# A quarter of the down projection by seven block products in place of eight

## The chip, the cores and the metric

The kernel runs on one core of a Trainium2 chip. The metric is the device time of one launch in microseconds (us), as the median of several runs. The engines are named as in the profile: PE is TensorE (PEld its weight loads), DVE is VectorE, ACT is ScalarE, POOL is GpSimd and SP is SyncE, whose queue issues the loads.

## The reference

One layer of an encoder trunk on 256 tokens of width 2048, in float32. After a combined input projection, three branches (a bidirectional state-space scan, a dilated windowed attention, a convolution module) are gated and merged. Then follows the part that this case is about, the MLP with 8192 hidden columns:

```python
x = x + merged @ w_out[i]
h2 = rms_norm(x, norm2_g[i])
x = x + jnp.square(jax.nn.relu(h2 @ w_mlp_up[i])) @ w_mlp_down[i]
```

## The kernel before

All large products are made in one stream of *units*. A unit is 256 rows of a weight matrix times 512 output columns: one load of 128 x 1024 floats (512 KB, tile `raw`, five buffers). Every operand is carried as two parts of type `fp32r`: ACT copies `raw` into `hi`, and DVE subtracts to make `lo = raw - hi` (`split_lo`, L254). Both have four buffers, and `split` runs `LEAD` = 3 units ahead of the matmuls (`mm`). A product a x w is then three matmuls: a_hi w_hi and a_lo w_hi (first all those that read `hi`), then a_hi w_lo.

In a unit of the down projection ("X" mode) the activations are the stationary operand: the 256 rows are two chunks e of 128, the 256 tokens two halves t, so 2 x 2 x 3 = 12 matmuls of 512 columns. They accumulate in a `main` tile of two PSUM banks (one for each t). In the up projection ("W" mode) the weights are stationary, 24 matmuls of 256 columns.

A *block* is eight units with one accumulator: 2048 rows of K, 512 output columns. The MLP is cut into r = 0 to 3, each with 2048 hidden columns: four up blocks ("U", r, i), then four down blocks ("D", r, i) over K of 2048, in the order U0 U1 D0 U2 D1 U3 D2 D3. When an up block is done, `job_up` has DVE apply relu and the norm (`u`, L1075, two instructions), ACT square it and copy it to `ah`, and DVE split off `al`. When a down block is done, `job_down` adds its two banks into `oacc[i]` (tile `x` in the traces) on DVE (L1095), or for r = 3 adds and stores the output (L1099).

What the engines do in which order is fixed when the program is built. The loop over units writes down, for unit k, the load of k + 5, the split of k + 3 and the matmuls of k. Then `S.tick` lets waiting jobs write some of their instructions, against a credit of free DVE and ACT time. Each engine executes its own queue in order and waits on semaphores. PSUM has eight banks: the pool `pm` gives two `main` tiles (four banks), the pool `pd` four single banks for everything else; the last block of all takes two of `pd`. `S.require` makes the planner write a reader's instructions before the buffer is given out again.

Of the kernel before, what the change touches and what calls it, by code (L numbers as in the profile page):

```python
# [12 lines left out]
F32 = mybir.dt.float32  # L13
# [7 lines left out]
P = 128  # L21
# [169 lines left out]
def kernel(ctx: ExitStack, tc: tile.TileContext, xT, xn, par, cm, cd, cq, w1, wq, ws, out):  # L191
# [869 lines left out]
        st["rbc2"] = rb  # L1061


    act = {}

    def job_up(main, r, i):
        yield "m", 3
        u = slab([4, T], name="u")
        h = slab([4, T], F32R, name="ah")
        l = slab([4, T], F32R, name="al")  # L1070
        yield "j", lambda: "rbc2" in st
        yield "w", 1
        for e in range(2):
            yield "v", 680
            V.scalar_tensor_tensor(u[:, 2 * e:2 * e + 2, :], main[:, e, :].rearrange("p (a b) -> p a b", a=2), 0.0,  # L1075
                                   st["rbc2"][:, None, :].to_broadcast([P, 2, T]), op0=ALU.max, op1=ALU.mult)
        st["main_free"].add(id(main))
# [7 lines left out]
        S.give()  # L1085
        act[r][0][i] = h
        act[r][1][i] = l

    def job_down(main, r, i):
        if r < 3:  # L1090
            yield "j", lambda: oacc[i] is not None
            yield "w", 1
            for t in range(2):
                yield "v", 620
                V.tensor_tensor(oacc[i][:, t, :], oacc[i][:, t, :], main[:, t, :], op=ALU.add)  # L1095
            st["main_free"].add(id(main))
            return
        for t in range(2):
            V.tensor_tensor(oacc[i][:, t, :], oacc[i][:, t, :], main[:, t, :], op=ALU.add)  # L1099
            (nc.sync, nc.scalar)[t].dma_start(out[t * P:t * P + P, i * 512:i * 512 + 512], oacc[i][:, t, :])  # L1100
        st["main_free"].add(id(main))
        yield "w", 0


    st.update(h=([None] * 4, [None] * 4), ssd=([None] * 4, [None] * 4), conv=([None] * 4, [None] * 4),
              main_free=set(), conv_t=set(), q_blocks=0, att_n=0, ssd_c=[0] * 4, ssd_n=0, z_n=0, z_g=[False] * 4, mg_n=0,
              mgp=([None] * 4, [None] * 4), x2g=([None] * 4, [None] * 4))
    yss = cp.tile([P, 2, 4], F32, name="yss")
    st["yss"] = yss
# [67 lines left out]
    def up_block(r, i):  # L1177
        act.setdefault(r, ([None] * 4, [None] * 4))
        block("W", lambda: st["x2g"], lambda m: [(job_up(m, r, i), 0)],
              end=(lambda: S.give(8)) if (r == 3 and i == 3) else None)  # L1180

    def down_block(r, i):
        block("X", lambda: act[r], lambda m: [(job_down(m, r, i), 0)],
              end=(lambda: S.give(8)) if i == 3 else None)

    for o in ORDER:
        k, i = o[0], int(o[1])
# [7 lines left out]
        (up_block if k == "U" else down_block)(r, i)  # L1195


    units = [(bi, u) for bi, b in enumerate(blocks) for u in range(b["units"])]
    NU = len(units)
    raws, his, los = {}, {}, {}  # L1200

    def load(k):
        if k >= NU:
            return
        bi, u = units[k]
# [10 lines left out]
        raws[k] = t  # L1216

    def split(k):
        if k >= NU:
            return  # L1220
        bi, u = units[k]
        n = 2 * blocks[bi]["n"]
        h = hp.tile([P, 1024], F32R, tag="hi", name=nm("hi"))[:, :n]
        l = lp.tile([P, 1024], F32R, tag="lo", name=nm("lo"))[:, :n]
        r = raws.pop(k)
        if k == 0:
            for e in range(2):
                es = slice(e * n // 2, (e + 1) * n // 2)
                prep(e)
                A.activation(h[:, es], r[:, es], AF.Copy)  # L1230
                split_lo(l[:, es], r[:, es], h[:, es])
        else:
            A.activation(h, r, AF.Copy)  # L1233
            split_lo(l, r, h)
        his[k], los[k] = h, l
        S.on_split(k, n / 1024)

    mains = {}

    class Pair:  # L1240
# [5 lines left out]
        def __getitem__(self, at):  # L1246
            return self.of[at[1]][:, at[2]]

    def mm(k):
        bi, u = units[k]  # L1250
        b = blocks[bi]
        n, nk = b["n"], 2 * b["units"]
        if u == 0:
            if bi >= 2:
                j = mains[bi - 2]
                S.require(lambda: id(j) in st["main_free"], f"block {bi - 2} read")
                st["main_free"].discard(id(j))
            mains[bi] = pm.tile([P, 2, 512], F32, tag="main", name=nm("main")) if bi + 1 < len(blocks) \
                else Pair(bank(), bank())
        main = mains[bi]  # L1260
        wh = his.pop(k).rearrange("p (a b) -> p a b", a=2)
# [12 lines left out]
        first, last = kcs[0] == 0, kcs[1] == nk - 1  # L1274
        tail = bi == len(blocks) - 1 and u == b["units"] - 1
        order = [(ps, e, kc, t) for ps in range(2) for e, kc in enumerate(kcs) for t in range(2)]
        if tail:
            order.sort(key=lambda o: o[3])
        for ps, e, kc, t in order:
            ah, al = hi[kc // 4][:, kc % 4, :], lo[kc // 4][:, kc % 4, :]  # L1280
            if b["mode"] == "W":
                for c in (2 * t, 2 * t + 1):
                    o = main[:, t, (c % 2) * T:(c % 2) * T + T]
                    cs = slice(c * P, c * P + P)
                    if ps == 0:
                        PE.matmul(o, wh[:, e, cs], ah, start=(first and e == 0 and c % 2 == 0), stop=False,  # L1286
                                  skip_group_check=True)
                        PE.matmul(o, wh[:, e, cs], al, start=False, stop=False, skip_group_check=True)  # L1288
                    else:
                        PE.matmul(o, wl[:, e, cs], ah, start=False, stop=(last and e == 1), skip_group_check=True)  # L1290
            else:
                o = main[:, t, :n]
                xs_ = slice(t, T, 2) if b["perm"] else slice(t * P, t * P + P)
                if ps == 0:
                    PE.matmul(o, ah[:, xs_], wh[:, e, :], start=(first and e == 0), stop=False)  # L1295
                    PE.matmul(o, al[:, xs_], wh[:, e, :], start=False, stop=False)  # L1296
                else:
                    PE.matmul(o, ah[:, xs_], wl[:, e, :], start=False, stop=(last and e == 1))  # L1298
        if u == b["units"] - 1:
            if b["end"]:  # L1300
                b["end"]()
            for g, pr in b["post"](main):
                S.add(g, f"block{bi}", pr)

    S.take(8)
    st["xg"] = ([slab([4, T], F32R, name="xgh") for _ in range(4)], [slab([4, T], F32R, name="xgl") for _ in range(4)])
# [17 lines left out]
    S.add(job_h(), "h", 0)  # L1324
    for k in range(NU):
        load_x(k + 5)
        load(k + 5)
# [93 lines left out]
```

## Time and profile before

| | |
|---|---|
| median of three runs | 1962.76 us (1962.56 to 1964.62) |
| profiled execution: its own time | 1963.07 us |
| its span, first to last instruction | 1961.3 us |
| mean granted TensorE clock | 0.998 |
| PE, PEld, DVE, ACT, POOL busy | 1951.5, 1757.7, 1303.2, 1017.1, 60.1 us |
| loads of 512 KB (`raw<-ws_dram`) | 600, 3.3 us from issue to landing |

In a profile row stand the line of the kernel, the engine, the operation, the output and input tiles, and the shape. Behind the bar of a group are its busy time and the mean duration in ns, then the idle time of the engine ahead of it and what ended that. In rows of the timeline the first number is the start, the second the duration, and the bracket holds the idle time ahead and its releaser. A matmul's row is longer than the distance to the next one, since matmuls are pipelined: the pace is read from the starts. Rows of stretches give the busy time of PE, PEld, DVE, ACT and POOL, then the granted clock, the share of the DMA engines and GB/s.

### The profile page before, as it was taken

How to read it: one execution, taken by the hardware profiler on the slowest of the kernel's cores; microseconds unless marked ns; L12 is line 12 of the kernel's file. 1: busy time of each engine (PE TensorE's matmuls, PEld its weight loads, DVE VectorE, ACT ScalarE, POOL GpSimd, SP SyncE). 2: the span in 40 equal slices, each digit the busy share in tenths (PEclk: the TensorE clock that was granted, in tenths of full speed). 3: DMA queues.
4: the chain of work that ended last, by engine and by line, in shares of the span. 5: the costliest groups of instructions: out<-in, count | busy, mean ns of one | idle time of the engine just before them, and what ended most of it. 6: DMA issues, size and time to landing. Idle time of an engine off the chain costs nothing.

```text
span 1961.3 us, 29893 instructions
## 1 busy us (share of the span) xinstructions
PE 1951.5 (100%) x11738; PEld 1757.7 (90%) x11738; DVE 1303.2 (66%) x1878; ACT 1017.1 (52%) x1386; POOL 60.1 (3%) x74
## 2 busy tenths in 40 slices
PE   9999999999999999999999999999999999999999
PEld 9899999999989888888888888999988998998887
DVE  6689887888887898887655555555554554555444
ACT  6665576666666645545554444544443443344332
POOL 0000010000000000003000000000000000000000
PEclk9999999999999999999999999999999999999999
DMA  8565565565555555555655556555555555555554
GB/s 329 163 219 188 164 193 184 174 198 177 194 189 188 183 193 182 184 192 183 193 192 184 190 194 205 187 190 184 187 189 191 185 185 192 192 183 191 185 182 151
DMA packets 108174, 373.03 MB, mean 190 GB/s; under 512 B 12288, under 2 KB 13056, under 8 KB 108032
## 3 DMA queue, kind: packets, MB, share of 16 engines
q1 hardware_dynamic: 103904, 360.23, 55.4%
q0 software_dynamic: 2560, 8.39, 1.6%
q10 hardware_dynamic: 1568, 2.49, 0.3%
q8 instruction: 92, 1.51, 0.3%
q14 instruction: 50, 0.41, 0.1%
HBM read 368.84 MB, written 2.23 MB: 189 GB/s over the span
## 4 chain that ended last, share of the span: by engine, by line
PE 98%; ACT 0%; DVE 0%; issue 0%; DMA 0%; SPq 0%; DVEq 0%; ACTq 0%
PE main L1295 20%; PE main L1296 20%; PE main L1298 20%; PE main L1288 11%; PE main L1286 11%; PE main L1290 11%; PE b L886 1%; PE b L990 1%; PE b L1296 0%; PE b L1295 0%; PE b L1298 0%; PE b L849 0%; PE b L523 0%; DVE lo L254 0%; ACT hi L1233 0%
## 5 line engine op out<-in xcount | busy, mean ns | idle before, releaser
L254 DVE TENSOR_TENSOR lo<-raw,hi 128x1024 fp32r<-128x1024 f32 (+2 forms) x697 | 831.7, 1194 | 629.3 <-ACT hi L1233 626.2
L1233 ACT ACTIVATE hi<-raw 128x1024 fp32r<-128x1024 f32 (+2 forms) x695 | 715.3, 1031 | 866.8 <-PE main L1296 481.9
L1295 PE MATMUL main<-hi,hh 128*128 128x512 f32 (+1 forms) x800 | 304.3, 380 | 0.0
L1296 PE MATMUL main<-hi,hl 128*128 128x512 f32 (+1 forms) x800 | 297.3, 372 | 0.0
L1286 PE MATMUL main<-x2h,hi 128*128 128x256 f32 x1024 | 247.7, 281 | 0.0
L1288 PE MATMUL main<-x2l,hi 128*128 128x256 f32 x1024 | 246.9, 281 | 0.0
L1286 PE MATMUL main<-hh,hi 128*128 128x256 f32 x896 | 218.3, 283 | 0.0
L1288 PE MATMUL main<-hl,hi 128*128 128x256 f32 x896 | 216.4, 281 | 0.0
L592 DVE SCALAR_TENSOR_TENSOR co<-cin,cpar,co 128x256 f32<-128x256 f32 x480 | 208.5, 487 | 0.0
L1298 PE MATMUL main<-lo,hh 128*128 128x512 f32 (+1 forms) x800 | 200.0, 372 | 0.0
L1288 PEld LDWEIGHTS main<-x2l,hi 128*128 128x128 f32 x1024 | 193.2, 189 | 0.1
L1286 PEld LDWEIGHTS main<-x2h,hi 128*128 128x128 f32 x1024 | 192.7, 188 | 0.2
L1296 PE MATMUL main<-hi,al 128*128 128x512 f32 x480 | 188.9, 394 | 0.0
L1295 PE MATMUL main<-hi,ah 128*128 128x512 f32 x480 | 188.6, 393 | 0.0
L1295 PEld LDWEIGHTS main<-hi,hh 128*128 128x128 f32 x800 | 152.3, 190 | 22.4 <-ACT hi L1233 1.0
L1296 PEld LDWEIGHTS main<-hi,hl 128*128 128x128 f32 x800 | 152.4, 191 | 21.9 <-issue 1.6
L1286 PEld LDWEIGHTS main<-hh,hi 128*128 128x128 f32 x896 | 170.3, 190 | 0.0
L1288 PEld LDWEIGHTS main<-hl,hi 128*128 128x128 f32 x896 | 170.3, 190 | 0.0
L1298 PEld LDWEIGHTS main<-lo,hh 128*128 128x128 f32 x800 | 147.8, 190 | 21.1
L1290 PE MATMUL main<-x2h,lo 128*128 128x256 f32 x1024 | 141.5, 281 | 0.0
L1298 PE MATMUL main<-lo,ah 128*128 128x512 f32 x480 | 130.0, 393 | 0.0
L1290 PEld LDWEIGHTS main<-x2h,lo 128*128 128x128 f32 x1024 | 129.7, 189 | 0.0
(241 smaller groups left out, 2254.0 us busy)
## 6 DMA issues: line engine op xcount, KB each, us to landing
raw<-ws_dram SPq DMA_DIRECT2D x600, 512.0 KB, 3.3
raw<-wq_dram SPq DMA_DIRECT2D x88, 384.0 KB, 3.1
fr<-sums POOLq DMA_DIRECT2D x32, 256.0 KB, 5.8
raw<-w_dram SPq DMA_DIRECT2D x7, 448.0 KB, 6.8
xr<-xn_dram SPq DMA_DIRECT2D x4, 512.0 KB, 8.0
x<-xn_dram SPq DMA_DIRECT2D x4, 512.0 KB, 4.5
xt<-xT_dram SPq DMA_DIRECT2D x7, 256.0 KB, 6.8
out_dram<-x SPq DMA_DIRECT2D x4, 256.0 KB, 3.8
```

Source lines behind the costliest of these rows:

```text
L254: V.tensor_tensor(lo, raw, hi.bitcast(F32), op=ALU.subtract)
L592: V.scalar_tensor_tensor(dst[:, e, :], x[:, e, k:k + T], par_("dw", (2 * i + e) * 31 + k), dst[:, e, :], op0=ALU.mult, op1=ALU.add)
L886: PE.matmul(bd[:, i, :], em[:, 0, i, :], x[:, c, pr:pr + P], start=True, stop=True)
L990: PE.transpose(b[:, e, t * P:t * P + P], src[:, t, k * P:k * P + P], ID)
L1233: A.activation(h, r, AF.Copy)
L1286: PE.matmul(o, wh[:, e, cs], ah, start=(first and e == 0 and c % 2 == 0), stop=False, skip_group_check=True)
L1288: PE.matmul(o, wh[:, e, cs], al, start=False, stop=False, skip_group_check=True)
L1290: PE.matmul(o, wl[:, e, cs], ah, start=False, stop=(last and e == 1), skip_group_check=True)
L1295: PE.matmul(o, ah[:, xs_], wh[:, e, :], start=(first and e == 0), stop=False)
L1296: PE.matmul(o, al[:, xs_], wh[:, e, :], start=False, stop=False)
L1298: PE.matmul(o, ah[:, xs_], wl[:, e, :], start=False, stop=(last and e == 1))
```

## The change

The down blocks are taken two at a time, D(r, i) with D(r, i+1) for i = 0 and 2, as one block of mode "Y" with 16 units. Of its K of 2048 rows a quarter, two steps u = 0 and 1 of 256 rows, is multiplied differently. In a step the activations are a 2 x 2 arrangement of 128 x 128 pieces (two halves t, two chunks e) and the weights 2 x 2 pieces of 128 x 512 (two chunks, two blocks). The eight block products of that are replaced by seven (Winograd's form of Strassen's scheme). For it,

- `job_up` makes four sums of activation pieces for each r (`sf`, with the parts `sh` and `sl`), from the first up block;
- `split` makes four sums of weight pieces a step in a slab `us` (L1332), two for the unit "b" and two, written over those, for the unit "c";
- the seven products of a step are the units "a", "b", "d", "c" with 2, 2, 1, 2 products of three matmuls each; "a" and "d" split loaded pieces, "b" and "c" split sums;
- three products accumulate directly in the two blocks' accumulators, four in four further banks ("four"), which `job_seven` unloads into `oacc` with one ACT copy and eight DVE adds behind the pair.

The units of a pair come in the order: u = 2, 3 of the first block, u = 2, 3 of the second, the eight small units, u = 4 to 7 of the first block, u = 4 to 7 of the second. A pair with i = 0 has its accumulators in `pm` and the four further banks in `pd`; with i = 2 it is the other way round. Up blocks with r > 0 and i = 2, 3 take their accumulators from `pd` ("apart").

```diff
@@ job_up
+        if i == 0:
+            yield "m", 3
+            f = slab([4, 2, P], name="sf")
...
+                yield "v", 400
+                V.tensor_tensor(f[:, o], x, y_, op=op)
...
+            A.activation(sh, f, AF.Copy)
...
+            split_lo(sl, f, sh)
+            acs[r] = sh, sl
@@ new
+    def job_seven(p, done, i):
+        p1, p5, p6, p7 = p
+        yield "m", 1
+        tq = slab([2, 512], name="tq")
...
+        A.activation(tq[:, 0, :], p1, AF.Copy)
...
+        V.tensor_tensor(c11, c11, p1, op=ALU.add)
+        V.tensor_tensor(tq[:, 0, :], tq[:, 0, :], p6, op=ALU.add)
+        V.tensor_tensor(tq[:, 1, :], p5, tq[:, 0, :], op=ALU.subtract)
+        V.tensor_tensor(c21, c21, p7, op=ALU.add)
+        V.tensor_tensor(c22, c22, p7, op=ALU.subtract)
+        done()
+        for c, e in ((c21, 0), (c12, 1), (c22, 1)):
+            V.tensor_tensor(c, c, tq[:, e, :], op=ALU.add)
@@ the list of units
+        for e, us in ((0, (2, 3)), (1, (2, 3)), (None, (0, 1)), (0, (4, 5, 6, 7)), (1, (4, 5, 6, 7))):
+            for u in us:
+                if e is None:
+                    order_ += [(bi, u), (bi, 8 + u)]
+                    for w in "abdc":
+                        units.append((bi, u, w, (len(order_) - 2, len(order_) - 1)))
...
@@ split
+                if w == "b":
...
+                    sums[u] = slab([1024], name="us")
+                    todo = ((0, x[:, :512], y_[:, :512]), (512, y_[:, :512], y_[:, 512:]))
+                else:
+                    todo = ((0, sums[u][:, :512], y_[:, 512:]), (512, sums[u][:, :512], x[:, 512:]))
+                r = sums[u]
+                for o, p, q in todo:
+                    V.tensor_tensor(r[:, o:o + 512], p, q, op=ALU.add)
             A.activation(h, r, AF.Copy)
             split_lo(l, r, h)
@@ seven (matmuls of the small units)
+        todo = {"a": ((A_(0, 0), f1, 0), (A_(1, 0), c1, 0)), "b": ((S_(1), f1, 1), (S_(3), f2, 1)),
+                "d": ((S_(4), c2, 0),), "c": ((S_(2), f2, 0), (A_(1, 1), c1, 1))}[w]
+        for ps in range(2):
+            for i, ((xh, xl), o, t) in enumerate(todo):
+                cs = slice(512 * i, 512 * i + 512)
...
+                if ps == 0:
+                    PE.matmul(o[:, t, :], xh, wh[:, cs], start=(four and u == 0), stop=False)
+                    PE.matmul(o[:, t, :], xl, wh[:, cs], start=False, stop=False)
+                else:
+                    PE.matmul(o[:, t, :], xh, wl[:, cs], start=False, stop=(four and u == 1))
```

How this moves the queues is seen on DVE at the quarter of the first pair with i = 2 (r = 0). In the program before, DVE's queue in the middle of D(0, 2) holds one split a unit:

```order
L254 TENSOR_TENSOR lo_14280<-raw_14241,hi_14279 128x1024
L254 TENSOR_TENSOR lo_14298<-raw_14259,hi_14297 128x1024
L254 TENSOR_TENSOR lo_14316<-raw_14277,hi_14315 128x1024
L254 TENSOR_TENSOR lo_14334<-raw_14295,hi_14333 128x1024
L254 TENSOR_TENSOR lo_14352<-raw_14313,hi_14351 128x1024
```

In the changed program the second step of that quarter stands there like this on DVE, from the split of unit "c" of the first step on (`us` are the weight sums):

```order
L254 TENSOR_TENSOR lo_14336<-us_14298,hi_14335 128x1024
L254 TENSOR_TENSOR lo_14350<-raw_14315,hi_14349 128x1024
L1332 TENSOR_TENSOR us_14361<-raw_14315,raw_14317 128x512
L1332 TENSOR_TENSOR us_14361<-raw_14317 128x512
L254 TENSOR_TENSOR lo_14360<-us_14361,hi_14359 128x1024
L254 TENSOR_TENSOR lo_14372<-raw_14317,hi_14371 128x512
L1332 TENSOR_TENSOR us_14361<-us_14361,raw_14317 128x512
L1332 TENSOR_TENSOR us_14361<-us_14361,raw_14315 128x512
L254 TENSOR_TENSOR lo_14384<-us_14361,hi_14383 128x1024
```

Two splits for two units of 12 matmuls have become four splits and four sums for units of 6, 6, 3 and 6 matmuls, and a sum stands in the queue behind the split of the unit ahead of it.

On ACT the same place, before and then after:

```order
L1233 ACTIVATE hi_14279<-raw_14241 128x1024
L1233 ACTIVATE hi_14297<-raw_14259 128x1024
L1233 ACTIVATE hi_14315<-raw_14277 128x1024
L1233 ACTIVATE hi_14333<-raw_14295 128x1024
L1233 ACTIVATE hi_14351<-raw_14313 128x1024
```

```order
L1333 ACTIVATE hi_14335<-us_14298 128x1024
L1333 ACTIVATE hi_14349<-raw_14315 128x1024
L1333 ACTIVATE hi_14359<-us_14361 128x1024
L1333 ACTIVATE hi_14371<-raw_14317 128x512
L1333 ACTIVATE hi_14383<-us_14361 128x1024
```

Two of the four copies of a step now read what DVE has written (`us`), where all of them read a loaded tile before.

At the first pair of a round, here r = 0, the end of the up projection's work stands ahead of the quarter in DVE's queue (`u` and `al` belong to the last up block):

```order
L1080 SCALAR_TENSOR_TENSOR u_13924<-b_13681,rbc_12157 128x512
L1080 SCALAR_TENSOR_TENSOR u_13924<-b_13682,rbc_12157 128x512
L254 TENSOR_TENSOR lo_13948<-raw_13892,hi_13947 128x1024
L254 TENSOR_TENSOR al_13926<-u_13924,ah_13925 128x1024
L1332 TENSOR_TENSOR us_13968<-raw_13892,raw_13894 128x512
L1332 TENSOR_TENSOR us_13968<-raw_13894 128x512
L254 TENSOR_TENSOR lo_13966<-us_13968,hi_13965 128x1024
```

The split `al` stands between the split of unit "a" and the sums for unit "b"; before, it stood between two plain splits.

More of the change, by code (lines that the diff above doesn't have):

```diff
@@ L1061, in job_rms2, with free @@
         st["rbc2"] = rb
-    act = {}
+    act, acs = {}, {}
+    def free(main):
+        st["main_free"].add(id(main))
+        if isinstance(main, Pair):
+            S.banks += 2
     def job_up(main, r, i):
@@ L1089, in job_down @@
+        S.give()
     def job_down(main, r, i):
+        yield "j", lambda: oacc[i] is not None
         if r < 3:
-            yield "j", lambda: oacc[i] is not None
             yield "w", 1
-            for t in range(2):
+        else:
+            yield "j", lambda: st["seven"] >= 7 + i // 2
+        for t in range(2):
+            if r < 3:
                 yield "v", 620
-                V.tensor_tensor(oacc[i][:, t, :], oacc[i][:, t, :], main[:, t, :], op=ALU.add)
-            st["main_free"].add(id(main))
@@ L1180, in up_block @@
               end=(lambda: S.give(8)) if (r == 3 and i == 3) else None)
+        blocks[-1]["apart"] = r > 0 and i >= 2
     def down_block(r, i):
-        block("X", lambda: act[r], lambda m: [(job_down(m, r, i), 0)],
-              end=(lambda: S.give(8)) if i == 3 else None)
+        if i % 2 == 0:
+            block("Y", lambda: act[r], None, units=16)
+            blocks[-1].update(r=r, i=i)
     for o in ORDER:
@@ L1195, with load_upto @@
         (up_block if k == "U" else down_block)(r, i)
-    units = [(bi, u) for bi, b in enumerate(blocks) for u in range(b["units"])]
-    NU = len(units)
-    raws, his, los = {}, {}, {}
+    units, order_ = [], []
+    for bi, b in enumerate(blocks):
+        if b["mode"] != "Y":
+            for u in range(b["units"]):
+                order_.append((bi, u))
+                units.append((bi, u, "n", (len(order_) - 1,)))
+            continue
+        for e, us in ((0, (2, 3)), (1, (2, 3)), (None, (0, 1)), (0, (4, 5, 6, 7)), (1, (4, 5, 6, 7))):
[5 more added lines that the diff above has]
+                else:
+                    order_.append((bi, 8 * e + u))
+                    units.append((bi, u + 8 * e, "n", (len(order_) - 1,)))
+    NU, NR = len(units), len(order_)
+    raws, his, los = {}, {}, {}
+    read = set()
+    loaded = [0]
+    def load_upto(k):
+        top = units[min(k, NU - 1)][3][-1]
+        while loaded[0] <= top and (loaded[0] < 5 or loaded[0] - 5 in read):
+            load(loaded[0])
+            loaded[0] += 1
     def load(k):
-        if k >= NU:
-            return
-        bi, u = units[k]
+        bi, u = order_[k]
         b = blocks[bi]
@@ L1232, in split @@
         else:
+            if w in "na":
+                r = raws[rs[0]]
+            elif w == "d":
+                r = raws[rs[1]][:, 512:]
+            else:
+                x, y_ = raws[rs[0]], raws[rs[1]]
+                if w == "b":
+                    S.require(lambda: S.mem >= 1, "slab for sums")
+                    S.take()
+                    sums[u] = slab([1024], name="us")
+                    todo = ((0, x[:, :512], y_[:, :512]), (512, y_[:, :512], y_[:, 512:]))
+                else:
+                    todo = ((0, sums[u][:, :512], y_[:, 512:]), (512, sums[u][:, :512], x[:, 512:]))
+                r = sums[u]
+                for o, p, q in todo:
+                    V.tensor_tensor(r[:, o:o + 512], p, q, op=ALU.add)
             A.activation(h, r, AF.Copy)
             split_lo(l, r, h)
+        if w == "c":
+            S.give()
+        if w in "nc":
+            read.update(rs)
+            for i in rs:
+                raws.pop(i)
         his[k], los[k] = h, l
[L1236 removed]
+        S.on_split(k, n / 1024 if w not in "bc" else 2.0)
     mains = {}
@@ L1247, in __getitem__, with pm_tile, pd_pair @@
             return self.of[at[1]][:, at[2]]
+    pms = []
+    def pm_tile():
+        if len(pms) >= 2:
+            j = pms[-2]
+            S.require(lambda: id(j) in st["main_free"], "accumulators read")
+            st["main_free"].discard(id(j))
+        pms.append(pm.tile([P, 2, 512], F32, tag="main", name=nm("main")))
+        return pms[-1]
+    def pd_pair():
+        S.require(lambda: S.banks >= 2, "banks read")
+        S.banks -= 2
+        return Pair(bank(), bank())
     def mm(k):
-        bi, u = units[k]
+        bi, u, w, _ = units[k]
         b = blocks[bi]
         n, nk = b["n"], 2 * b["units"]
[L1253 to L1259, printed above, removed]
+        pair = b["mode"] == "Y"
+        if bi not in mains:
+            if pair:
+                S.require(lambda: b["r"] in acs, "sums of activations")
+                make = pm_tile if b["i"] == 0 else pd_pair
+                mains[bi] = [make(), make()]
+            else:
+                mains[bi] = (pd_pair if b.get("apart") else pm_tile)()
+        if w != "n":
+            if (u, w) == (0, "a"):
+                make = pd_pair if b["i"] == 0 else pm_tile
+                b["four"] = [make(), make()]
+            seven(k)
+            return
         main = mains[bi]
+        if pair:
+            j, u = divmod(u, 8)
+            main = main[j]
+            nk = 16
         wh = his.pop(k).rearrange("p (a b) -> p a b", a=2)
@@ L1273, in mm @@
         hi, lo = parts(b["key"])
-        first, last = kcs[0] == 0, kcs[1] == nk - 1
-        tail = bi == len(blocks) - 1 and u == b["units"] - 1
+        first, last = kcs[0] == (4 if pair else 0), kcs[1] == nk - 1
+        tail = k == NU - 1
         order = [(ps, e, kc, t) for ps in range(2) for e, kc in enumerate(kcs) for t in range(2)]
@@ L1298, in mm @@
                     PE.matmul(o, ah[:, xs_], wl[:, e, :], start=False, stop=(last and e == 1))
-        if u == b["units"] - 1:
+        if pair:
+            if u == 7:
+                if j == 1 and b["i"] == 2:
+                    S.give(8)
+                S.add(job_down(main, b["r"], b["i"] + j), "down", 0)
+        elif u == b["units"] - 1:
             if b["end"]:
@@ L1303, in mm, with seven, done @@
                 S.add(g, f"block{bi}", pr)
+    def seven(k):
+        bi, u, w, _ = units[k]
+        b = blocks[bi]
+        (ah, al), (sh, sl) = [[x[0] for x in act[b["r"]]], acs[b["r"]]]
+        wh, wl = his.pop(k), los.pop(k)
+        S.on_mm(k, 0.25 if w == "d" else 0.5)
+        c1, c2 = mains[bi]
+        f1, f2 = b["four"]
+        A_ = lambda e, t: (ah[:, 2 * u + e, t * P:t * P + P], al[:, 2 * u + e, t * P:t * P + P])
+        S_ = lambda i: (sh[:, i - 1, u, :], sl[:, i - 1, u, :])
+        todo = {"a": ((A_(0, 0), f1, 0), (A_(1, 0), c1, 0)), "b": ((S_(1), f1, 1), (S_(3), f2, 1)),
[3 more added lines that the diff above has]
+                cs = slice(512 * i, 512 * i + 512)
+                four = o is f1 or o is f2
+                if ps == 0:
+                    PE.matmul(o[:, t, :], xh, wh[:, cs], start=(four and u == 0), stop=False)
+                    PE.matmul(o[:, t, :], xl, wh[:, cs], start=False, stop=False)
+                else:
+                    PE.matmul(o[:, t, :], xh, wl[:, cs], start=False, stop=(four and u == 1))
+        if (u, w) == (1, "c"):
+            if b["i"] == 2:
+                S.give(2)
+            def done():
+                for o in b["four"]:
+                    free(o)
+            S.add(job_seven((f1[:, 0, :], f1[:, 1, :], f2[:, 0, :], f2[:, 1, :]), done, b["i"]), "seven", 0)
     S.take(8)
```

59 lines of the change are left out of this document (43 added, 16 removed).

## The prediction

> **What bounds the kernel now.** I read the engine table of the page first, then the chain that ended last, the busy time in stretches, the waits, and then the instructions of the down projection one by one.
>
> ```profile
> PE 1951.5 (100%) x11738; PEld 1757.7 (90%) x11738; DVE 1303.2 (66%) x1878; ACT 1017.1 (52%) x1386; POOL 60.1 (3%) x74
> PE 98%; ACT 0%; DVE 0%; issue 0%; DMA 0%; SPq 0%; DVEq 0%; ACTq 0%
> 80.00:90.00 10.00, 7.40 (x40) 7.06 (x41) 4.94 (x12) 7.27 (x21) 0.00 (x0) 0.66 0.37 127
> ...
> 1800.00:1900.00 100.00, 100.00 (x433) 81.04 (x432) 49.50 (x46) 37.67 (x36) 0.00 (x0) 1.00 0.55 184
> DVE lo L254 <- ACT hi L1233: 626.2, 529, 3.6
> ACT hi L1233 <- PE main L1296: 481.9, 306, 4.4
> ```
>
> TensorE is never idle in the down projection: busy for all of 1800 to 1900 us at full clock, while DVE works 50% and ACT 38% of it. The waits run backwards: ACT copies (hi) wait for PE to give a buffer back, and DVE (lo) waits for ACT. So today a matmul saved is time saved, and the other two engines have slack. The slack is only there on the average, though: a look at one plain unit shows how it is made up.
>
> ```profile
> 1829.02 1.06 ACT L1233 ACTIVATE hi<-raw 128x1024 fp32r<-128x1024 f32 x1 [1.74 <-PE main L1296]
> 1830.11 1.22 DVE L254 TENSOR_TENSOR lo<-raw,hi 128x1024 fp32r<-128x1024 f32 x1 [1.58 <-ACT hi L1233]
> 1831.37 0.40 PE L1296 MATMUL main<-hi,al 128*128 128x512 f32 x1
> 1831.80 1.06 ACT L1233 ACTIVATE hi<-raw 128x1024 fp32r<-128x1024 f32 x1 [1.73 <-PE main L1296]
> L1295 PE MATMUL main<-hi,ah x128: 387/392/404, 1421.4 to 1509.1; 128*128 128x512 f32 x128
> L1295 PE MATMUL main<-hi,ah x128: 387/389/396, 1601.1 to 1687.7; 128*128 128x512 f32 x128
> ```
>
> PE's last use of a hi buffer ends at 1831.77 and ACT refills it at 1831.80: a hop of 0.03 us. ACT's end at 1830.08 and DVE's start at 1830.11 give the same hop. A unit of 12 matmuls takes (1509.1 - 1421.4) / 31.5 = 2.78 us in the first down projection and 2.75 in the second (128 rows are 32 units, the last row stands in the middle of its unit): 0.231 us a matmul. DVE needs 1.23 of those 2.8 us, ACT 1.06.
>
> **What goes.** Per pair of blocks, two steps u of K take 21 matmuls in place of 24. Eight pairs: 8 x 2 x 3 = 48 matmuls, 48 x 0.231 = 11.1 us off PE, all on the path.
>
> **What comes, and where it lies.** The seven products need five more things, priced by these rows.
>
> ```profile
> L254 DVE TENSOR_TENSOR lo<-raw,hi 128x1024 fp32r<-128x1024 f32 x600 | 738.0, 1231 | 578.0 <-ACT hi L1233 576.5
> L879 DVE TENSOR_TENSOR em<-em 128x512 f32<-128x512 f32 x16 | 11.1, 692 | 3.2 <-ACT em L872 1.6 <-ACT co L587 0.5
> L996 DVE TENSOR_TENSOR ml<-b,mh 128x512 fp32r<-128x512 f32 x8 | 5.5, 684 | 0.0
> L1233 ACT ACTIVATE hi<-raw 128x1024 fp32r<-128x1024 f32 x600 | 634.9, 1059 | 813.0 <-PE main L1296 450.7 <-PE main L1288 274.9 <-DVE co L592 26.1
> L1047 ACT ACTIVATE sq<-x 128x512 f32<-128x512 f32 x8 | 5.0, 628 | 0.0
> L1095 DVE TENSOR_TENSOR x<-x,main 128x512 f32<-128x512 f32 x24 | 15.3, 681 | 0.0
> L891 DVE TENSOR_TENSOR y<-y,b 128x256 f32<-128x256 f32 x16 | 6.6, 415 | 0.0
> raw<-ws_dram SPq DMA_DIRECT2D x600, 512.0 KB, 3.3
> 1274.70 1.22 DVE L254 TENSOR_TENSOR lo<-raw,hi 128x1024 fp32r<-128x1024 f32 x1 [1.66 <-ACT hi L1233]
> ```
>
> 1. Four weight sums a step on DVE, 128x512 from SBUF: 0.69 each (L879, the same form).
> 2. Splits of seven half tiles, not four: three of 1024 and one of 512 (0.68 on DVE, 0.63 on ACT). DVE then has 3 x 1.23 + 0.68 + 4 x 0.69 = 7.1 us a step, while PE has 21 x 0.231 = 4.85. Inside the stretch DVE is the larger, so this is where the path can change hands.
> 3. The unloading of the four product banks: one ACT copy and eight DVE adds, 0.6 + 8 x 0.68 = 6 us a pair. They stand among the plain units behind the stretch, where DVE is idle 1.58 us in 2.8; eight units give 12.6 us against 6 + 2.7 for four ordinary adds. Nothing, as long as the banks are back eight units later.
> 4. The sums of activations, once for each r: 4 x 0.42 + 1.23 on DVE and 1.06 on ACT, among up-projection units, where DVE idles 1.66 us in a unit (1274.70), and used 24 units or more later. Nothing.
> 5. Loads: the same 600 of 512 KB. Two raw buffers stay taken through a step, and the next two loads start together when its last sum has read them; at 3.3 us to landing they are there more than 5 us before their unit. SP has only loads behind them. Nothing. Were late loads not covered, the next hi copies would wait.
>
> The shared banks add waits for a reader at three first uses a round: a block's accumulators and the four banks were read out at least four units (11 us) earlier in program order. Nothing, bounded by one 0.68 read each, 8 x 0.7 = 5 us, if they came last.
>
> **The stretch worked through.** Names: units a, b, d, c of step 0, then a', b', d', c' of step 1; 6, 6, 3, 6 matmuls each, plain units before and behind. There are still four hi and four lo buffers, so the hi of a unit can start only when PE has done with the hi of the unit four before. Against rows on which spacing and restarts rest:
>
> ```profile
> 1255.63 0.16 DVE L272 RECIPROCAL rr<-rs 128x2 f32<-128x2 f32 x1
> 1255.83 0.16 DVE L276 TENSOR_TENSOR rs<-rr 128x2 f32<-128x2 f32 x1
> ...
> 1263.29 1.23 DVE L254 TENSOR_TENSOR lo<-raw,hi 128x1024 fp32r<-128x1024 f32 x1 [2.04 <-ACT hi L1233]
> 1264.43 1.28 DVE L1075 SCALAR_TENSOR_TENSOR u<-main,rbc 128x512 f32<-128x512 f32 x2
> ```
>
> ```profile
> 5.96 0.58 ACT L1230 ACTIVATE hi<-raw 128x448 fp32r<-128x448 f32 x1 [1.19 <-DMA raw<-w_dram]
> 6.59 0.29 PEld L1295 LDWEIGHTS main<-hi,xgh 128*128 128x128 f32 x1 [0.92 <-ACT hi L1230]
> 1830.21 0.19 PEld L1296 LDWEIGHTS main<-hi,al 128*128 128x128 f32 x1
> ```
>
> A DVE instruction that waits for nothing starts 0.09 us before the one ahead ends (1264.43 against 1263.29 + 1.23); one that reads its predecessor's result starts 0.04 after it (1255.79 to 1255.83). PE held by a hi copy begins with the weight load 0.05 after it (6.54 to 6.59) and at full clock needs 0.19 for it, so the first matmul runs 0.25 after the copy.
>
> Time 0 is the first matmul of a. Its fourth, the last that reads hi, starts at 0.69 and ends at 1.08. From there: hi a' 1.11 to 2.17; lo a' 2.20 to 3.43; its two sums for b' 3.34 to 4.63; hi b' 4.67 to 5.73; lo b' 5.76 to 6.99; lo d' to 7.59; the first sum for c' 7.50 to 8.19, the second, which reads the first's output, 8.23 to 8.92; hi c' 8.96 to 10.02; lo c' 10.05 to 11.28. Without waits PE would be at c' after 36 matmuls, at 8.32. It can start at 10.27: a wait of 1.95. Its fifth matmul then wants lo at 11.19 and gets it at 11.53: 0.34 more. So 2.29 us lost, against 6 x 0.231 = 1.39 won. What is late next: nothing. The following plain units have hi at 11 and lo at 12.4, ahead of their turn, and DVE catches up.
>
> In the first stretch of r = 0 and r = 1 the order of DVE puts the last lo of the up projection (al, 1.23 us, itself waiting for two ACT passes) ahead of the sums for b. That shifts hi c to 1.93 and with it, on ACT, hi a' from 2.17 to 2.90, and lo a' ends 0.9 later; b' then waits 0.64 + 0.34 and c' ends 0.9 later: 3.19 us. For r = 2 al stands behind the lo of b and costs nothing in the end; r = 3 has down units ahead.
>
> Sum: 6 x 2.29 + 2 x 3.19 = 20.1 us of waits, less 11.1: +9.0. On the profiled execution, 1963.07 us with a span of 1961.3, that is 1972.1. The median of the three runs is 0.3 lower, so 1971.8.
>
> Bounds of the uncertain prices. If DVE and ACT never overlapped neighbours, the same recurrence gives 24.6 us of waits: +13.5. A restart at the bare hop of 0.03 gives 18.5: +7.4; with that half way and an overlap of 0.12 it is 16.9: +5.6. I take the middle, since each link has a row of its own kind. This case's own range is 1968 to 1977.
>
> On the overlap, the Trainium skill's "VectorE: DVE Perf Modes", section "The DRAIN you can't avoid", says that the next Vector instruction does not start until the pipe is empty. By that rule the sum is the +13.5 just given (1976); the pair at 1264.43, 1.28 us for two, disagrees, and I go by the row.
>
> **Rivals.**
>
> *The chain keeps up (faster).* Place: the ten links from the release of a's hi to the hi of c'. It decides at a wait of 1.39 us a stretch, 0.9 less than I find; for 0.2% in time it must be 1.4 us shorter, 0.14 a link. Then about 1959; with no wait at all 1963.07 - 11.1 = 1952. For it: unheld neighbours do overlap by 0.09. Against: in this chain nearly every link waits for another engine, and waiting rows show the full 1.06 and 1.23. 8%.
>
> *An even game.* Waits of 0.9 to 1.9 us a stretch, from prices all at their low ends: 1959 to 1966.7. 12%.
>
> *The clock drops.* PE gaps of 2 us may lower the granted clock. The start-up shows gaps in these rows:
>
> ```profile
> PE b L395 <- issue: 2.3, 1, 2.3
> PE b L523 <- ACT qn L508: 2.0, 2, 1.5
> 70.00:80.00 10.00, 8.32 (x71) 7.93 (x69) 6.16 (x15) 5.41 (x19) 0.00 (x0) 1.00 0.43 141
> ```
>
> The 1.5 us gap left the clock at 1.00 in 70 to 80; behind the 2.3 us gap, with 2.0 us of gaps shortly before it, it was 0.66 in 80 to 90, which is 10 x 0.34 = 3.4 us of clock. My gap of 1.95, with 0.34 after it, lies between. If every second stretch paid 3.4 us: 1972 + 13.6 = 1985. Against: gaps stand some 45 us apart or more, with PE full between them. 14%. The Trainium skill's "TensorE: Matmul & The Clock Gate", section "What's actually happening", asks for an idle window of about 3.4 us before the clock halves; by it gaps of 2 us would leave the time at 1972, while the trace's own drop came with no gap longer than 2.3.
>
> **How the numbers follow.** The likeliest case has 66%. The three runs of this kernel span 0.1%, so about 0.2% (3.9 us) can be told from no change. Faster 0.08 and the even game 0.12 as above; the likeliest and the clock are slower, 0.80. The range from 1963.5, into the even game, to 1984, into the clock's case, leaves out about 2 in 10.
>
> **What would show it.** In the changed kernel PE is idle about 2 us once in each of eight stretches, ahead of the c' matmuls, waiting for ACT's hi, that one waiting for DVE's sum; twice also ahead of b'. DVE is busy nearly throughout a stretch or waits there for ACT, and no idle time stands at the bank reads. Wrong, if PE has no gaps (then 1952), if gaps also appear at plain units (loads or banks are late), or if the granted clock falls behind them.

## The result, and the profile after

| | before | after |
|---|---|---|
| median | 1963.14 us (1962.56 to 1964.62, 4 runs) | 1979.06 us (1978.20 to 1981.09, 4 runs) |
| ratio | | 1.0083 (1.0070 to 1.0096) |
| profiled execution: time, span | 1963.07, 1961.3 | 1978.20, 1976.4 |
| mean granted clock | 0.998 | 0.996 |

The changed kernel is slower by 15.9 us. The forecast was +9.0, 1971.8 in a range of 1963.5 to 1984.

First the engine table, the chain that ended last, the same 100 us as before in stretches, and the waits (engine, tile and line, what it waited for: us in all, times, longest):

```profile
PE 1949.5 (99%) x11690; PEld 1747.7 (88%) x11690; DVE 1416.9 (72%) x2058; ACT 1046.5 (53%) x1430; POOL 60.2 (3%) x74
PE 93%; DVE 3%; ACT 2%; issue 1%; DMA 0%; SPq 0%; ACTq 0%; DVEq 0%
1800.00:1900.00 100.00, 95.80 (x408) 75.71 (x406) 76.87 (x88) 43.94 (x47) 0.00 (x0) 1.00 0.53 179
PEld b L1459 <- ACT hi L1333: 10.5, 6, 2.1
PEld main L1459 <- ACT hi L1333: 8.4, 4, 2.1
PEld b L1462 <- DVE lo L254: 3.6, 8, 0.5
PEld main L1462 <- DVE lo L254: 3.3, 8, 0.5
```

PE lost its 48 matmuls (11738 to 11690), and the path left PE for 7% of the span: DVE 3, ACT 2, issue 1. All these waits are in the small units (L1459 reads hi, L1462 reads lo): ten for a hi, at most 2.1 us (eight c' and two b'), and sixteen for a lo, at most 0.5 (every c' and every b'). DVE's busy time in the stretch rose from 49.5 to 76.9 us in 100, still far from full. An average of 77% hides that it comes too late for one unit out of the twenty of a pair.

That unit, c' in the first pair with i = 2 (timeline of DVE and ACT, then of PE; the stretch begins with the first matmul of a at 1478.14):

```profile
1478.14 0.39 PE L1459 MATMUL main<-hi,ah 128*128 128x512 f32 x1
...
1479.31 1.06 ACT L1333 ACTIVATE hi<-raw 128x1024 fp32r<-128x1024 f32 x1 [0.48 <-PE b L1460]
1480.41 1.23 DVE L254 TENSOR_TENSOR lo<-raw,hi 128x1024 fp32r<-128x1024 f32 x1 [0.32 <-ACT hi L1333]
1481.55 0.68 DVE L1332 TENSOR_TENSOR us<-raw,raw 128x512 f32<-128x512 f32 x1
1482.15 0.68 DVE L1332 TENSOR_TENSOR us<-raw 128x512 f32<-128x512 f32 x1
1482.95 1.06 ACT L1333 ACTIVATE hi<-us 128x1024 fp32r<-128x1024 f32 x1 [2.58 <-DVE us L1332]
...
1484.04 1.22 DVE L254 TENSOR_TENSOR lo<-us,hi 128x1024 fp32r<-128x1024 f32 x1 [1.21 <-ACT hi L1333]
1485.18 0.68 DVE L254 TENSOR_TENSOR lo<-raw,hi 128x512 fp32r<-128x512 f32 x1
1485.79 1.41 DVE L1332 TENSOR_TENSOR us<-us,raw 128x512 f32<-128x512 f32 x2
1487.31 1.06 ACT L1333 ACTIVATE hi<-us 128x1024 fp32r<-128x1024 f32 x1 [2.78 <-DVE us L1332]
```

```profile
1486.35 0.40 PE L1462 MATMUL b<-lo,sh 128*128 128x512 f32 x1
1488.42 0.50 PE L1459 MATMUL main<-hi,sh 128*128 128x512 f32 x1 [1.67 <-ACT hi L1333]
...
1489.21 0.40 PE L1460 MATMUL b<-hi,al 128*128 128x512 f32 x1
1489.68 0.80 PE L1462 MATMUL main<-lo,sh 128*128 128x512 f32 x1
```

Read it from the top: hi a' starts only at 1479.31, on PE's release of a's buffer; then each row waits for the one above it, alternately on ACT and DVE, down to hi c', which ends at 1488.37. PE's last matmul of d' started at 1486.35 and c' could have followed at 1486.58. It starts at 1488.42, 1.84 later, and its fifth matmul is late by another 0.24 for its lo.

Then the clock. Three of the eight stretches are followed by some 3.4 us at half clock (granted clock in the third column from the right; first a window with the gap and the one behind it; then the windows behind the other two such gaps; last a gap with no drop behind it):

```profile
1486.27:1489.68 3.41, 1.67 (x8) 0.72 (x6) 2.17 (x4) 2.37 (x3) 0.00 (x0) 1.00 0.58 210
1489.68:1493.09 3.41, 3.41 (x8) 2.74 (x9) 3.41 (x4) 2.96 (x4) 0.00 (x0) 0.50 0.61 216
...
1674.00:1677.40 3.40, 3.40 (x9) 2.62 (x8) 3.40 (x4) 2.62 (x4) 0.00 (x0) 0.50 0.67 219
1902.70:1906.10 3.40, 3.40 (x9) 2.65 (x9) 3.40 (x4) 2.46 (x4) 0.00 (x0) 0.50 0.67 223
1807.12:1810.53 3.41, 1.74 (x8) 1.13 (x7) 2.17 (x4) 1.62 (x2) 0.00 (x0) 1.00 0.38 107
1810.53:1813.94 3.41, 3.34 (x14) 2.38 (x14) 3.41 (x4) 3.41 (x5) 0.00 (x0) 1.00 0.63 231
```

In such a window PE is busy throughout and gets 8 or 9 matmuls done, where 3.4 us at full clock hold 15 (3.4 / 0.231): 1.7 us lost each time.

The account of the profiled execution. I take each stretch from its first matmul to the first plain one behind it and subtract 42 x 0.231. The six ordinary stretches lose 2.4 us where the clock stays, the first ones of r = 0 and 1 lose 3.4 and 3.5: 6 x 2.4 + 6.9 = 21.3. Three drops at 1.7 are 5.1. Less the 11.1 saved: +15.3, against 1976.4 - 1961.3 = 15.1 in the spans. The match is a little too good: the changed execution came to the down projection 0.9 us sooner (its first matmul at 1420.48 against 1421.37), and from there to its last two matmuls (1971.69 against 1956.55) it is 16.0 us longer, so some 0.7 us are not in the account.

### The profile page after: what moved, and what is told of

Its sections match the earlier page's. It is cut to its first block, busy times and chain, and to the rows that moved or that the text cites. A ratio compares the mean times of both kernels' runs of the same rounds, so it can differ in the third digit from the quotient of the medians.

```text
span 1976.4 us, 30082 instructions
## 1 busy us (share of the span) xinstructions
PE 1949.5 (99%) x11690; PEld 1747.7 (88%) x11690; DVE 1416.9 (72%) x2058; ACT 1046.5 (53%) x1430; POOL 60.2 (3%) x74
## 4 chain that ended last, share of the span: by engine, by line
PE 93%; DVE 3%; ACT 2%; issue 1%; DMA 0%; SPq 0%; ACTq 0%; DVEq 0%
PE main L1427 16%; PE main L1428 16%; PE main L1430 16%; PE main L1420 9%; PE main L1422 9%; PE main L1418 9%; PE b L1420 2%; PE b L1422 2%; PE b L1418 2%; PE b L1427 2%; PE b L1428 2%; PE b L1430 2%; ACT hi L1333 1%; DVE lo L254 1%; DVE us L1332 1%
## 5 line engine op out<-in xcount | busy, mean ns | idle before, releaser
L254 DVE TENSOR_TENSOR lo<-raw,hi 128x1024 fp32r<-128x1024 f32 (+3 forms) x697 | 820.0, 1181 | 496.6 <-ACT hi L1333 490.9
L1333 ACT ACTIVATE hi<-raw 128x1024 fp32r<-128x1024 f32 (+3 forms) x695 | 705.4, 1020 | 768.6 <-PE main L1428 342.4
L1418 PE MATMUL main<-x2h,hi 128*128 128x256 f32 x640 | 155.0, 281 | 0.0
L1420 PE MATMUL main<-x2l,hi 128*128 128x256 f32 x640 | 154.3, 281 | 0.0
L1422 PE MATMUL main<-hh,lo 128*128 128x256 f32 x896 | 123.6, 280 | 0.0
L1420 PEld LDWEIGHTS main<-x2l,hi 128*128 128x128 f32 x640 | 120.8, 189 | 0.2
L1418 PEld LDWEIGHTS main<-x2h,hi 128*128 128x128 f32 x640 | 120.4, 188 | 0.2
L1422 PEld LDWEIGHTS main<-hh,lo 128*128 128x128 f32 x896 | 113.2, 189 | 0.0
L1418 PE MATMUL b<-x2h,hi 128*128 128x256 f32 x384 | 92.8, 281 | 0.0
L1420 PE MATMUL b<-x2l,hi 128*128 128x256 f32 x384 | 92.6, 281 | 0.0
```

The lines of the kernel that those rows point to most:

```text
L254: V.tensor_tensor(lo, raw, hi.bitcast(F32), op=ALU.subtract)
```

## The experiments

Theory A: the second step of a pair comes before DVE has made up for the first, so that the chain through DVE and ACT sets c' (21 us), and the gaps lower the clock (5 us). Theory B: the time goes into what comes with the pairs in any case: banks, unloading, loads. Theory C: small units cost PE more in themselves. Each kernel was compared with the kernel before on the same chip.

**Pairs without the seven products.**

```diff
-        for e, us in ((0, (2, 3)), (1, (2, 3)), (None, (0, 1)), (0, (4, 5, 6, 7)), (1, (4, 5, 6, 7))):
+        for e, us in ((0, range(8)), (1, range(8))):
...
-        first, last = kcs[0] == (4 if pair else 0), kcs[1] == nk - 1
+        first, last = kcs[0] == 0, kcs[1] == nk - 1
```

> The pairs with their shared banks, the accumulators now in pm and now in pd, and the sums of activations stay; the seven products go: all K is multiplied in plain units, in the order u = 0 to 7 of the first block, then of the second. Theory A: all of this is hidden, as costed in the prediction at nothing: same time as before (1963), no PE gaps. Theory B: the banks or the sums of activations cost PE waits, and a good part of the 16 us is seen here.

Measured: 1964.28 us (11 runs) beside 1963.0, ratio 1.0006 (0.9997 to 1.0015). At the place of the first two pairs:

```profile
1420.00:1520.00 100.00, 100.00 (x478) 83.05 (x477) 50.76 (x48) 40.08 (x38) 0.00 (x0) 1.00 0.56 188
```

PE is busy for all of the 100 us. The pairs, the accumulators now in `pm` and now in `pd`, and the sums of activations cost nothing that can be told from zero, at most 0.15%; this part of theory B falls. The four further banks are not taken here; they stay in the experiments with two and one plain units below. In the profiled execution the down projection takes 0.9 us more than before (1421.63 to 1957.74), which could be the 0.7 us that the account above leaves open; no run shows it.

**The weight sums left out.**

```diff
-                r = sums[u]
-                for o, p, q in todo:
-                    V.tensor_tensor(r[:, o:o + 512], p, q, op=ALU.add)
+                r = x if w == "b" else y_
```

> The order of the changed kernel, but the four sums of weight pieces a step are left out: units b and c split a loaded tile in place of the sums (so other numbers are computed), everything else stands. Theory A: DVE has 3 x 1.23 + 0.68 = 4.4 us a step, below PE's 4.85, so the chain never falls behind: no gaps, clock as before, 1963 - 11.1 = 1952 us. Rival (the ring of four hi and lo buffers is too short for small units whatever DVE does): the gap at c' stays at a good part of 1.8 us and the time at 1965 or more. Theory B (banks, unloading, loads): near 1979 as now.

Measured: 1952.47 us, ratio 0.9947 (0.9932 to 0.9962). The same place as c' above, on DVE and ACT:

```profile
1481.92 1.23 DVE L254 TENSOR_TENSOR lo<-raw,hi 128x1024 fp32r<-128x1024 f32 x1 [0.26 <-ACT hi L1327]
1482.20 1.06 ACT L1327 ACTIVATE hi<-raw 128x1024 fp32r<-128x1024 f32 x1 [0.32 <-PE b L1454]
```

ACT again waits for PE, not PE for ACT. The four buffers are enough for small units once the sums are gone, the drops of the clock are gone with the gaps, and the whole 11 us shows. Units of 6 and 3 matmuls cost PE nothing extra: theory C falls.

**Two plain units between the steps.** Nothing is left out here; only the order of the units changes.

```diff
-        for e, us in ((0, (2, 3)), (1, (2, 3)), (None, (0, 1)), (0, (4, 5, 6, 7)), (1, (4, 5, 6, 7))):
+        for e, us in ((0, (2, 3)), (1, (2, 3)), (None, (0,)), (0, (4,)), (1, (4,)), (None, (1,)),
+                      (0, (5, 6, 7)), (1, (5, 6, 7))):
```

> The same work as in the changed kernel, but two plain units stand between the two seven-product steps of a pair. Theory A (the second step is late because DVE is still behind from the first; ACT and PE only pass that on): DVE needs 7.1 us for a step of 4.85 us and gets 2 x (2.75 - 1.23) = 3 us back in the two plain units, so PE finds hi and lo ready everywhere. No gap at c', no drop of the clock, and the whole saving of 48 x 0.231 = 11.1 us shows: about 1952 us where before is 1963, ratio 0.994. Theory B (the time goes into what comes with the pairs wherever the steps stand: the shared banks, the unloading of the four product banks, the loads that start two at a time): it stays near 1979. Theory C (small units cost PE more than their matmuls, by restarts and half tiles): in between, 1957 to 1970, with loss inside the steps but no gap at c'.

Measured: 1953.18 us (1952.43 to 1954.40), ratio 0.9951 (0.9938 to 0.9963), so it beats both kernels. Engine table, chain, 100 us, and PE at the c' of the first pair with i = 2:

```profile
PE 1938.8 (99%) x11690; PEld 1745.9 (90%) x11690; DVE 1415.5 (73%) x2058; ACT 1045.8 (54%) x1430; POOL 60.1 (3%) x74
PE 98%; DVE 1%; ACT 1%; issue 0%; DMA 0%; SPq 0%; DVEq 0%; ACTq 0%
1800.00:1900.00 100.00, 100.00 (x434) 81.13 (x433) 83.19 (x97) 46.93 (x49) 0.00 (x0) 1.00 0.58 196
```

```profile
1488.57 0.40 PE L1463 MATMUL b<-lo,sh 128*128 128x512 f32 x1
1488.81 0.40 PE L1460 MATMUL main<-hi,sh 128*128 128x512 f32 x1
```

The last matmul of d' and the first of c' stand 0.24 apart. DVE does the same 2058 instructions in the same 1416 us as in the changed kernel, and now PE waits for it and ACT only three times in the down projection, 0.9 us in all. This also ends theory B: unloading, loads, banks and sums are all still there, and hidden. What was wrong in the changed kernel was only where the work stood.

**One plain unit between the steps.**

```diff
-        for e, us in ((0, (2, 3)), (1, (2, 3)), (None, (0, 1)), (0, (4, 5, 6, 7)), (1, (4, 5, 6, 7))):
+        for e, us in ((0, (2, 3)), (1, (2, 3)), (None, (0,)), (0, (4,)), (None, (1,)),
+                      (0, (5, 6, 7)), (1, (4, 5, 6, 7))):
```

> One plain unit between the two steps of a pair, where the changed kernel has none and the spread one two. A dose for theory A: the unit gives DVE 1.5 us back and ACT's ring one more place, so of the 2.29 us of a stretch some 0.7 stay (0.35 at c' and 0.33 for its lo), 1.1 in the first stretch of r = 0 and 1: 6 x 0.68 + 2 x 1.09 = 6.3 us of waits, less 11.1, hence -4.9: 1958 us beside 1963. Gaps of 0.4 to 0.8 us leave the clock at 1.00. If the loss were a fixed price of two steps in one pair, it would be 1979; if any separation were enough, 1952.

Measured: 1963.11 us, ratio 0.9999 (0.9990 to 1.0008): between the two orders as theory A has it, but 5 us above the number expected. Its waits, and a c' in the second round:

```profile
PEld b L1460 <- ACT hi L1334: 5.1, 4, 1.8
PEld main L1460 <- ACT hi L1334: 3.5, 4, 0.9
```

```profile
1661.19 0.69 DVE L1333 TENSOR_TENSOR us<-raw 128x512 f32<-128x512 f32 x1
1662.00 1.06 ACT L1334 ACTIVATE hi<-us 128x1024 fp32r<-128x1024 f32 x1 [2.58 <-DVE us L1333]
...
1664.83 1.41 DVE L1333 TENSOR_TENSOR us<-us,raw 128x512 f32<-128x512 f32 x2
1666.36 1.06 ACT L1334 ACTIVATE hi<-us 128x1024 fp32r<-128x1024 f32 x1 [2.79 <-PE main L1463]
```

A pair loses 1.0 us six times, not 0.68, and 1.8 and 1.9 in the other two, not 1.09: 9.9 us of waits, not 6.3, and 9.9 - 11.1 = -1.2, beside -1.3 in the spans (1960.0 against 1961.3). Three small prices make the 0.3 to 0.4 of the six: the two sums for c' are held and take 1.41 (I had reckoned with 1.29 here, though the prediction had the held price); from the end of a sum to the start of the hi that reads it are 0.12 us (1661.88 to 1662.00, 1666.24 to 1666.36; the bracket of the second names a matmul that ended in between), not 0.04, twice; and c' loses 0.1 in its second matmul. For the two larger ones I have no row that explains all of it.

**Sums for b on POOL.**

```diff
-                    V.tensor_tensor(r[:, o:o + 512], p, q, op=ALU.add)
+                    (G if w == "b" else V).tensor_tensor(r[:, o:o + 512], p, q, op=ALU.add)
...
-        e, dv, da = {... "b": (0.5, 2.1, 1), ...}[w]
+        e, dv, da = {... "b": (0.5, 1, 1), ...}[w]
```

> The changed kernel's order, with the two weight sums for unit b made on POOL in place of DVE; the two for unit c stay on DVE. POOL's nearest rows are 1.47 us for a 128x512 product and 1.02 to 1.07 for a 128x256 sum, so 3 to 4 us for the pair of sums, beside a step of 4.85 us, and they need only the two loaded tiles. Theory A: DVE has 7.1 - 1.4 = 5.7 us a step, hi b' no longer waits for lo a' and the sums; hi c' then ends at 8.2 where PE is there at 8.3, its lo at 9.4 where 9.2 is wanted: 0 to 0.4 us a stretch, 1952 to 1956 us. Rival 1 (DVE and POOL slow each other, or POOL needs over 2 us a sum): hi b' is late instead, and the time is 1960 or more. Rival 2 (it is the ring of four buffers, not DVE's load): the gap at c' stays above 1 us, 1968 or more.

Measured: 1969.65 us, ratio 1.0033 (1.0022 to 1.0044), a miss by 14 us. The first stretch, and one of i = 2:

```profile
1434.97 1.23 DVE L254 TENSOR_TENSOR lo<-us,hi 128x1024 fp32r<-128x1024 f32 x1 [1.19 <-ACT hi L1333]
...
1436.28 2.22 POOL L1332 TENSOR_TENSOR us<-raw,raw 128x512 f32<-128x512 f32 x1 [6.77 <-DVE lo L254]
1438.46 1.26 POOL L1332 TENSOR_TENSOR us<-raw 128x512 f32<-128x512 f32 x1
1439.75 1.06 ACT L1333 ACTIVATE hi<-us 128x1024 fp32r<-128x1024 f32 x1 [3.86 <-POOL us L1332]
...
1440.86 0.50 PE L1459 MATMUL b<-hi,sh 128*128 128x512 f32 x1 [2.48 <-ACT hi L1333]
...
1482.35 1.31 POOL L1332 TENSOR_TENSOR us<-raw 128x512 f32<-128x512 f32 x1
1482.42 2.32 DVE L254 TENSOR_TENSOR lo<-us,hi 128x1024 fp32r<-128x1024 f32 x1 [1.21 <-ACT hi L1333]
```

In the first stretch of r = 0 and 1 POOL stood idle for 6.77 us, waiting for DVE to read the last sum of the step before (the lo that ended at 1436.20); only then could it write the next. The sums need a free tile for `us` besides the two loaded tiles, which the expectation had left out; in these two stretches none was free earlier, elsewhere one was. PE then waited 2.48 us for hi b', the clock fell (0.50 from 1441.84 to 1448.67), and these two stretches lost 6.7 and 6.0 us. Where POOL could start early (five of the other six stretches) only 0.2 to 0.6 us was lost, so taking 1.4 us of a step's 7.1 off DVE does remove the gap at c' there, and Rival 2, in whose range the time lies, is not the cause there. The last stretch lost 1.5; DVE's pair of sums for c stood beside POOL's sums there and took 2.50 us in place of 1.41, and no run tests whether that is all of it. The 2.32 us of the split at 1482.42 are 1.23 and a wait for POOL, whose sum ended at 1483.66. The Trainium skill's "SBUF — State Buffer", section "Who interferes with whom", says that a Vector instruction with two SBUF inputs and a GpSimd instruction that reads SBUF block each other and the later one waits; the row agrees (1483.66 to its end at 1484.74 are 1.08), and so does POOL's sum at 1436.28, 2.22 us beside a split. All eight make 16.1 us, less 11.1: +5.0, beside +5.1 in the spans (1966.4 against 1961.3).

**The gap filled.**

```diff
+        if (u, w) == (1, "c"):
+            for _ in range(FILL):
+                PE.matmul(c2[:, 0, :], zero, st["dhi"][:, :512], start=False, stop=False)
```

> The changed kernel with eight more matmuls ahead of the c' unit of each pair, a stationary of zeros times the hi of d', added into an accumulator (adds nothing). They take 8 x 0.231 = 1.85 us, the length of the gap, so c' is not later than now but PE is not idle ahead of it. Theory A with the clock: the three stretches of 3.4 us at half clock, 1.7 us each, come from the gaps, so the clock stays at 1.00 in all of the down projection and the time falls from 1979 to about 1974, the mean clock from 0.996 back to 0.998. Rival (the drops have another cause, such as the load on the chip in the denser stretch): the drops stay and the time is 1979. If the fillers come out longer than the gap, up to 0.2 us a pair is added.

Measured: 1974.46 us (1973.75 to 1974.91), ratio 1.0059 (1.0045 to 1.0072). A gap, now filled, and the window behind it:

```profile
1487.99 2.03 PE L1459 MATMUL b<-hi,zero 128*128 128x512 f32 x8
1489.85 0.46 PE L1465 MATMUL main<-hi,sh 128*128 128x512 f32 x1
...
1489.70:1493.10 3.40, 3.33 (x15) 2.34 (x14) 3.30 (x3) 3.40 (x5) 0.00 (x0) 1.00 0.66 251
```

c' is no earlier than it was, but the clock stays at 1.00 and 4.6 us come back. The drops are caused by the idle time.

**A quarter of the gap filled** (FILL = 2).

> As with the eight fillers, but only two matmuls on zeros ahead of c', 0.46 us: a gap of 1.4 us of idle PE stays in each stretch, and 0.4 us of short waits behind it. By the threshold of about 2 us of idle time in one window of 3.4 us no drop of the clock is left, and the time is that of eight fillers, 1974. If a gap of 1.4 us is enough to halve the clock at times, it lies between 1974 and 1979.

Measured: 1974.50 us, ratio 1.0058 (1.0041 to 1.0075), and the whole of the down projection at full clock:

```profile
1420.00:1960.00 540.00, 528.49 (x3017) 456.09 (x3016) 377.61 (x413) 244.53 (x249) 0.00 (x0) 1.00 0.55 182
```

Shortening the idle time by 0.46 us a stretch is enough: a gap of 1.4 us with the short waits behind it never lowered the clock in eight stretches.

**The changed kernel once more**, nothing edited.

> The changed kernel once more, nothing edited, for the clock. In its first profile three of the eight gaps were followed by 3.4 us at half clock, and these stretches began 412.9 and 228.7 us before the last of them, which is 121 and 67 times 3.413. Theory of fixed windows: the activity is counted in windows of 3.41 us that run on whatever the kernel does, and a drop follows where about 2 us of idle time fall into one window: then drops come at other gaps this time, again at distances of multiples of 3.413 us, and only where the whole gap lies in one window (two to four of eight). Rival: the drops belong to certain stretches, those in 1478, 1662 and 1890: then they stand there again. The time moves with the number of drops, 1.7 us each: 1974 + 1.7 n.

Measured: 1978.48 us in one run, with three drops. They came at other stretches (first a window with the gap and the one behind it; then the windows behind the other two such gaps; last a gap without a drop):

```profile
1623.86:1627.28 3.42, 1.70 (x7) 0.79 (x6) 2.18 (x4) 2.48 (x3) 0.00 (x0) 1.00 0.67 232
1627.28:1630.69 3.41, 3.41 (x9) 2.64 (x10) 3.41 (x4) 2.85 (x4) 0.00 (x0) 0.50 0.60 199
1855.97:1859.38 3.41, 3.41 (x10) 2.63 (x9) 3.41 (x4) 2.59 (x4) 0.00 (x0) 0.50 0.66 233
1948.13:1951.54 3.41, 3.41 (x9) 2.64 (x10) 3.41 (x4) 2.83 (x4) 0.00 (x0) 0.50 0.61 214
...
1487.33:1490.74 3.41, 1.90 (x7) 1.30 (x8) 2.21 (x3) 3.08 (x4) 0.00 (x0) 1.00 0.77 270
1490.74:1494.16 3.42, 3.42 (x17) 2.74 (x16) 3.42 (x4) 3.20 (x4) 0.00 (x0) 1.00 0.67 210
```

None of the three stands where one stood before (1489.7, 1674.0, 1902.7), so the drops do not belong to stretches. Their distances are 228.7 and 92.2 us, that is 67.0 and 27.0 times 3.413; in the first profile 184.3 and 228.7, 54.0 and 67.0 times, and the drop of the start-up there (83.39) lies 412.0 times ahead of the first of them. With windows of that length laid out from the drops, seven of the sixteen gaps lie whole or nearly so in one window (1.66 us or more of the 1.84), four in the first execution and three in the second; the other nine are cut by a border. None of the nine lowered the clock: PE was busy 1.90 us or more in each of their windows (1487.33 above is the one with 1.90). Of the seven, six did, with PE busy 1.67 to 1.70 us in the window; the seventh is that of 1807.12, with 1.74. The idle time in the six is 1.71 to 1.74 us, less than the 2 us of the expectations. So what counts is how much of the idle time falls into one window, and not which stretch it is.

## Why the prediction was right, and where its size was off

*What goes* held: with the gaps gone (the spread order, the sums left out) the gain is 9.8 and 10.5 us of the 11.1 reckoned.

*Items 3 to 5 and the banks, costed at nothing,* held: the spread order keeps them all and has 0.9 us of waits in all; the pairs alone are at 1.0006 (0.9997 to 1.0015).

*The chain of a stretch* held, link by link. Counted from the first matmul of a at 1478.14, hi a' came at 1.17 (1.11 forecast), lo a' at 2.27 (2.20), hi b' at 4.81 (4.67), lo b' at 5.90 (5.76), the pair of sums for c' from 7.65 to 9.06 (7.50 to 8.92), hi c' at 9.17 (8.96), and the first matmul of c' at 10.28 (10.27). The last agrees so well because two errors cancel: each hop from a sum to its hi takes 0.1 and not 0.04, and PE starts its first matmul 0.05 after hi c' (1488.37 to 1488.42) and not 0.25; 0.10 of that shows up as a longer second matmul. The held pair of 1.41 us came out as forecast (8.92 - 7.50 = 1.42).

*DVE's overlap:* the second sum starts at 1482.15, 0.08 us before the first ends at 1482.23, as the row of before had it. The Trainium skill's "VectorE: DVE Perf Modes", section "The DRAIN you can't avoid", says that the next instruction waits for the empty pipe, but goes on: "A next op that is not held starts earlier". The rows agree with that second sentence, which the prediction had left out when it set the row against the page.

*The term of the waits* was 20.1 us and measured 21.3: 2.4 for 2.29, and 3.4 to 3.5 for 3.19. Every b' also waits a little for its lo, which the forecast had in two stretches only.

*The term that was mis-sized is the clock.* I costed it at nothing in the sum and kept it as a rival, "If every second stretch paid 3.4 us", with 14%. The mechanism is real; the price in it was not. The sum is wrong at this step: the prediction read the start-up by the length of single gaps, and what counted here is how much of one window of 3.41 us PE is idle (in the start-up of before, PE was busy only 1.24 us from 78.45 to 81.87, just ahead of the drop). Its own sign of being wrong, a granted clock that falls behind the gaps, is what came. Three drops in eight stretches is near every second one, but a window of 3.4 us at half clock loses 1.7 us and not 3.4: 5.1 us, not 13.6. The start-up's 3.4 was the price of two windows, 81.87 to 88.69; behind c' it is one each time. This and the 1.2 us of waits make up 6.3 of the 6.9 us between +9.0 and +15.9; the other 0.6 is no more than the runs spread. By the prediction's cases the outcome is the likeliest one with a milder form of its clock rival on top. The 1979.06 lies outside that case's own range of 1968 to 1977; it is in the stated range only because that reaches into the rival. Without drops (the gap filled) it is 1974.5, inside. How many drops a launch gets is not the program's doing, so the distance of 7 us to the forecast is partly chance. The Trainium skill's "TensorE: Matmul & The Clock Gate", section "What's actually happening", was weighed there as a rule by which no drop would come. The drops after gaps of 1.84 us go against its idle window of about 3.4 us; that its windows run freely, 3413 ns long, agrees with the distances measured.

*The rival that the chain keeps up* named the right point of decision. It put an even game at 1.39 us of waits a stretch. The order with one plain unit has 1.2 on average and comes out even (0.9999), and plain units between the steps are what moves it: one gives 1963, two give 1953.

## What to carry to other kernels

When work moves from the bounding engine to one with slack, do not compare averages but run the stretch through link by link: here DVE was 77% busy and still late for one unit of twenty, and the same instructions spread two units apart turned +15.9 us into -9.8. Put two bursts on a helper engine as far apart as it needs to catch up, (7.1 - 4.85) us of arrears against 1.5 us regained a plain unit. And price a gap on TensorE for more than its length: where about 1.7 us of idle time fell into one window of 3.41 us, it cost another 1.7 here, in three of eight stretches each time.

## What was not expected of the hardware

The granted clock halved for one window of 3.41 us when PE had been busy for only about half of the window before: 1.67 to 1.70 us in the six cases, while behind 1.74 and 1.90 us no drop came. The windows run on regardless of the program, as their distances show, so whether a gap of 1.84 us costs 1.7 us more depends on where a border falls: three of eight gaps in each of two profiled executions, and not the same three. Just where the edge lies stays open: the cases are few, the ends of matmuls are modelled, and at the end of the run with POOL a window with 1.63 us busy (1960.67 to 1964.08) was followed by no drop. That the drops come out of the idle time is shown by the fillers (1979.06 to 1974.46).
